# An encoder's first layer on Trainium2: the order of TensorE's instructions, once the planner's, is written out by hand

## The chip, the cores and the metric

The kernel runs on one core of a Trainium2 chip. The metric is the device time of one execution in microseconds (us). It was run three times, and once more with the hardware profiler, whose page and trace the sections below quote. A core has a matrix engine (TensorE, PE in the profile; its weight loads are listed apart as PEld), VectorE (DVE), ScalarE (ACT), GpSimd (POOL), the queues of SyncE (SP), from which all DMA transfers of this kernel are issued, and on-chip memory: SBUF, and PSUM, into which TensorE writes its products.

## What is computed

Two layers of a streaming encoder for one prompt of 1024 tokens and, beside it, 32 tokens of a second stream (the "sample") that has 512 cached keys and values. The width is 1024. Only the first layer is touched:

```python
# h: rmsnorm(x); proj = h @ w_in, 3072 columns: u, q, k, v, g_pool, g_att, 512 each
pool_out = scale * group_map(trailing_mean(u, 2 | 4 | 8 | 16) - u)   # 4 groups of 128 channels
# 8 heads of 64; chunks of 64 queries, each sees its own chunk and the 8 before it
s = einsum('cqhd,ckhd->hcqk', qc, kb) * 64 ** -0.5
s = where(key_chunk >= 0, s + bias[clip(distance, -128, 128)], -inf)
att = einsum('hcqk,ckhd->cqhd', softmax(s), vb)
mixed = concatenate([pool_out * silu(g_pool), att * silu(g_att)])
x = x + rmsnorm(mixed @ w_out)
...
# second layer: an mLSTM with matrix memory, chunk by chunk
```

## The kernel before

Everything is 32-bit. To multiply at TensorE's faster rate without losing accuracy, each operand of a projection is split into a high and a low part of 12 bits, and `mm3` (L99 to L108) adds three products: high by high (L106), low by high (L107) and high by low (L108). Channels lie on the partitions, tokens on the free axis, in three groups of 384, 384 and 288. A **step** is one tile of 128 output channels for one token group: 24 products into one PSUM tile `pd`, which has 3 buffers, and then an evacuation on VectorE or ScalarE. A **tile** of weights is three steps. It is loaded one tile ahead by `load_w`: a DMA into `wr`, the high part on ScalarE (L93), the low part in the first layer on GpSimd (L94), later on VectorE (L94).

The first layer (`layer0`) begins with the input's norm and the projections v and q of the first pair of heads. Then a loop runs over four pairs of heads (L628 to L663). In each pair, in the order of the program:

- what is left of the projection steps queued before (`fill_all`);
- `v_tokens` (L274): the values are turned to have tokens on the partitions, in nine transposes (L288) of a 128 by 128 block, four to a PSUM tile `pm` or `pv`; ScalarE (L289) copies each with a factor to the tile `vt`. Stores and loads of values go with it;
- stacked queries, the projection of the keys (three steps), stacked keys KA and KB, the near bias B;
- the gate `ga` (one buffer; evacuation L268: VectorE, ScalarE's tanh, VectorE), three steps;
- `PLAN` queues the projections v, q, u (pooling input) and gp (pooling gate) that come next, nine or twelve steps a pair;
- scores `att_s` for the two heads (e) and the two halves of the 1024 queries (hf). Scores of key block by queries are two products (L342, L343) into a PSUM tile `ps` (three buffers); two smaller key blocks share one tile (a bank). VectorE adds the near bias (L347), ScalarE the far one (L355). The result stands in `st` (four buffers). Then the maximum over the keys: VectorE's maxima (L363 to L371), an all-reduce over the partitions on GpSimd (L373), a subtraction on VectorE (L377) and the exp on ScalarE (L378);
- values `att_pv` (L388) into `pv` (one buffer), four products for the first half and eight for the second, taken out by ScalarE (L396, L397); behind the second head `att_out`: times the gate on GpSimd (L408), a reciprocal (L409) and a product on VectorE, and a store to `mix` in DRAM;
- the sample's own attention (`rest`, L425 to L462): scores into `ps`, the same steps of a softmax (all-reduce L441, exp L444), five values products (L454; the profile lists each twice, as it does those of L388 and L495) for each head into `pv`, each head's part read by VectorE (L456, L457), a transpose (L459) and a product with the gate.

Behind a tile u stand the trailing sums (`pool_sums`, GpSimd L477, VectorE L481 and L483), behind a tile gp the pooling product (`pool_mix`: L495 for three token groups on one PSUM tile `pm`, each read by VectorE, L497). The output projection (`out_proj`) reads `mix` back, splits the rows (L196) and follows.

None of this order is fixed on the engines. The whole is scheduled by a planner that simulates the kernel's time line and, on each engine, puts next what is ready by its reckoning, with earlier program text first. So projection steps lie among the attention's instructions in TensorE's queue wherever the planner put them, within a step too.

Of the kernel before, what the change touches and what calls it, by code (L numbers as in the profile page):

```python
# [33 lines left out]
class Net:  # L34
# [5 lines left out]
    # ---------------------------------------------------------------- consts  # L40
    def consts(self):
# [4 lines left out]
        # the table of the activations, before the data is there  # L46
# [24 lines left out]
    # keeps [s, t] with s <= t  # L71
# [4 lines left out]
    # ---------------------------------------------------------------- dense  # L76
# [40 lines left out]
    # the same, one token group at a time, to be put between other work; "make" gives evac when the tile starts  # L117
# [26 lines left out]
    # r = 1/sqrt(sum/1024 + eps), on all partitions, from per-partition sums; worked out with the tokens on the partitions  # L144
# [44 lines left out]
    # split x * g into two parts of 12 bits  # L189
# [15 lines left out]
    # the input: one group's tokens, with tiles that are not in use yet for what comes in  # L205
# [23 lines left out]
    # ---------------------------------------------------------------- layer 0  # L229
# [32 lines left out]
    # (1 + tanh(g/2)) * g, twice the silu  # L262
# [11 lines left out]
    def v_tokens(self, vT, pr):  # L274
# [8 lines left out]
        for b0 in (0, 4, 8):  # L283
# [6 lines left out]
        for e in range(2):  # L290
            c0 = pr * 128 + e * 64
            cs = slice(e * 128, e * 128 + 64)
            nc.sync.dma_start(out=io["vo"][0:512, c0:c0 + 64].rearrange("(b p) c -> p b c", p=128), in_=vt[:, 4:8, cs])
            nc.sync.dma_start(out=io["vo"][512:544, c0:c0 + 64], in_=vt[:DEC, 8, cs])
        return vt

    # hi and lo of both heads, stacked on the partitions
# [21 lines left out]

    def att_s(self, pr, e, hf, Q, KA, KB, B):  # L320
# [7 lines left out]
        for group in banks:  # L328
# [32 lines left out]
        mx = self.lp.tile([128, 512], F32, name="mx", bufs=2)  # L361
        if hf == 0:
            nc.vector.tensor_copy(out=mx[:, 0:128], in_=place[0][0][:, 0:128])  # L363
            nc.vector.tensor_tensor(out=mx[:, 128:512], in0=place[0][0][:, 128:512], in1=place[1][0], op=ALU.max)
            rest = [2, 3]
        else:
            nc.vector.tensor_tensor(out=mx, in0=place[3][0], in1=place[4][0], op=ALU.max)
            rest = [2, 1, 0, 5, 6, 7]
# [855 lines left out]
```

## Time and profile before

| | |
|---|---|
| time, three runs | 1272.14 us (median), 1271.83 to 1279.22 |
| span of the profiled execution | 1273.6 us, 19526 instructions |
| TensorE busy | 1200.1 us (94%) |
| TensorE's weight loads | 1148.3 us (90%), beside the products |
| VectorE, ScalarE, GpSimd busy | 688.7 (54%), 471.5 (37%), 316.3 us (25%) |
| DMA | 94.03 MB, mean 74 GB/s |
| chain that ended last | PE 77%, DVE 6%, issue 5%, DMA 5%, POOL 3%, ACT 2% |

The runs' times are the device's; the span is that of one execution under the profiler, and all rows further down are of that one. The chain that ended last is followed back from the last instruction to what released it, and so on; "issue" in it is time in which an engine waited for nothing that the profile shows. The first layer, to its output projection, fills some 460 us.

### The profile page before, as it was taken

How to read it: one execution, taken by the hardware profiler on the slowest of the kernel's cores; microseconds unless marked ns; L12 is line 12 of the kernel's file. 1: busy time of each engine (PE TensorE's matmuls, PEld its weight loads, DVE VectorE, ACT ScalarE, POOL GpSimd, SP SyncE). 2: the span in 40 equal slices, each digit the busy share in tenths (PEclk: the TensorE clock that was granted, in tenths of full speed). 3: DMA queues.
4: the chain of work that ended last, by engine and by line, in shares of the span. 5: the costliest groups of instructions: out<-in, count | busy, mean ns of one | idle time of the engine just before them, and what ended most of it. 6: DMA issues, size and time to landing. Idle time of an engine off the chain costs nothing.

```text
span 1273.6 us, 19526 instructions
## 1 busy us (share of the span) xinstructions
PE 1200.1 (94%) x7457; PEld 1148.3 (90%) x7457; DVE 688.7 (54%) x1457; ACT 471.5 (37%) x976; POOL 316.3 (25%) x409
## 2 busy tenths in 40 slices
PE   6998898978997979999999999999999999999996
PEld 6997797977897859999999989999999999998996
DVE  7654474564676644777435643574237532567324
ACT  6532333243443335543033423343224322346421
POOL 3222532342234223552010320021002210123232
PEclk9998988989999989999999989999999999999998
DMA  6311120111120225332111132113111311113323
GB/s 216 114 38 33 44 85 26 51 59 34 64 71 22 78 85 168 100 127 83 49 51 53 37 71 97 38 49 95 46 50 51 76 68 50 42 60 122 127 99 124
DMA packets 79613, 94.03 MB, mean 74 GB/s; under 512 B 19208, under 2 KB 56856, under 8 KB 79520
## 3 DMA queue, kind: packets, MB, share of 16 engines
q1 hardware_dynamic: 79520, 92.79, 23.5%
q8 instruction: 58, 0.95, 0.3%
q14 instruction: 35, 0.29, 0.1%
HBM read 72.64 MB, written 21.69 MB: 74 GB/s over the span
## 4 chain that ended last, share of the span: by engine, by line
PE 77%; DVE 6%; issue 5%; DMA 5%; POOL 3%; ACT 2%; SPq 0%; DVEq 0%; POOLq 0%; ACTq 0%
PE pd L107 20%; PE pd L106 20%; PE pd L108 20%; PE pv L388 3%; DMA xr<-mix 2%; PE pm L883 1%; PE ps L951 1%; PE ps L343 1%; PE ps L342 1%; POOL qT L477 1%; DMA wr<-in_w0o 1%; POOL wl L94 1%; PE pv L918 1%; DMA MA<-mdr 1%; PE pv L920 1%
## 5 line engine op out<-in xcount | busy, mean ns | idle before, releaser
L106 PE MATMUL pd<-xh,wh 128*128 128x384 f32 (+1 forms) x1864 | 613.6, 330 | 13.5 <-DVE ga L268 6.8
L107 PE MATMUL pd<-xl,wh 128*128 128x384 f32 (+1 forms) x1864 | 612.8, 329 | 13.9 <-POOL xl L196 9.5
L108 PE MATMUL pd<-xh,wl 128*128 128x384 f32 (+1 forms) x1864 | 612.7, 329 | 1.7 <-DVE wl L94 1.6
L107 PEld LDWEIGHTS pd<-xl,wh 128*128 128x128 f32 x1864 | 356.1, 191 | 19.1 <-POOL xl L196 10.2
L106 PEld LDWEIGHTS pd<-xh,wh 128*128 128x128 f32 x1864 | 356.2, 191 | 18.2 <-ACT wh L93 7.6
L108 PEld LDWEIGHTS pd<-xh,wl 128*128 128x128 f32 x1864 | 356.0, 191 | 5.2 <-DVE wl L94 3.0
L93 ACT CAST wh<-wr 128x512 fp32r<-128x512 f32 x158 | 91.4, 618 | 149.6 <-PE pd L107 122.4
L94 DVE TENSOR_TENSOR wl<-wr,wh 128x512 fp32r<-128x512 f32 x116 | 80.5, 718 | 23.7 <-ACT wh L93 22.1
L94 POOL TENSOR_TENSOR wl<-wr,wh 128x512 fp32r<-128x512 f32 x42 | 57.8, 1392 | 116.8 <-ACT wh L93 59.6
L187 POOL TENSOR_TENSOR acc<-acc,sqt 128x384 f32<-128x384 f32 (+1 forms) x48 | 56.6, 1178 | 92.2 <-ACT sqt L186 87.8
L388 PE MATMUL pv<-st,vt 128*128 128x512 f32 (+1 forms) x192 | 58.7, 448 | 0.2 <-ACT st L378 0.2
L73 POOL TENSOR_SCALAR_AFFINE_SELECT D<-D 128x128 f32<-128x128 f32 (+1 forms) x36 | 11.9, 331 | 180.8 <-ACT D L947 168.1
L388 PEld LDWEIGHTS pv<-st,vt 128*128 128x128 f32 x192 | 36.2, 195 | 20.7 <-issue 12.4
L963 POOL TENSOR_TENSOR qa<-qT,MA 128x128 f32<-128x128 f32 (+1 forms) x64 | 27.1, 441 | 107.1 <-DMA MA<-mdr 68.4
L965 POOL TENSOR_TENSOR qal<-qa,qah 128x256 fp32r<-128x256 f32 (+1 forms) x32 | 27.0, 847 | 103.9 <-ACT qah L964 91.6
L347 DVE TENSOR_TENSOR st<-ps,B 128x256 f32<-128x256 f32 (+1 forms) x72 | 26.1, 377 | 45.0 <-PE ps L343 44.4
L377 DVE TENSOR_TENSOR st<-st,mb 128x512 f32<-128x512 f32 (+1 forms) x96 | 40.0, 485 | 15.7 <-POOL mb L373 14.1
L256 DVE TENSOR_TENSOR row<-pd,r 128x384 f32<-128x384 f32 (+1 forms) x36 | 18.6, 521 | 54.4 <-PE pd L108 54.2
L983 DVE SCALAR_TENSOR_TENSOR C<-C,MA,ps 128x258 f32<-128x258 f32 x64 | 30.4, 478 | 32.2 <-PE ps L920 19.0
L373 POOL PARTITION_ALL_REDUCE mb<-mx x16 | 28.8, 1799 | 66.5 <-issue 25.2
L378 ACT ACTIVATE st<-st 128x1280 f32<-128x1280 f32 x24 | 30.4, 1272 | 31.2 <-DVE st L377 31.1
L355 ACT ACTIVATE st<-ps,far 128x256 f32<-128x256 f32 (+3 forms) x56 | 25.6, 487 | 38.9 <-DVE st L347 35.8
(306 smaller groups left out, 1675.8 us busy)
## 6 DMA issues: line engine op xcount, KB each, us to landing
wr<-in_w SPq DMA_DIRECT2D x128, 256.0 KB, 2.7
xr<-mix SPq DMA_DIRECT2D x26, 192.0 KB, 2.9
wr<-in_w0o SPq DMA_DIRECT2D x16, 256.0 KB, 3.1
MA<-mdr SPq DMA_DIRECT2D x32, 128.0 KB, 3.2
wr<-in_w1o SPq DMA_DIRECT2D x16, 256.0 KB, 3.2
x<-in_x SPq DMA_DIRECT2D x16, 192.0 KB, 2.8
x<-x1d SPq DMA_DIRECT2D x16, 192.0 KB, 3.8
out_y<-y SPq DMA_DIRECT2D x16, 192.0 KB, 2.1
```

Source lines behind the costliest of these rows:

```text
L93: nc.scalar.copy(out=wh[:, k], in_=wr)
L94: eng.tensor_tensor(out=wl[:, k], in0=wr, in1=wh[:, k].bitcast(F32), op=ALU.subtract)
L106: nc.tensor.matmul(out=p, lhsT=wh[:, k], rhs=xh[:, k], start=first and i == 0, stop=False)
L107: nc.tensor.matmul(out=p, lhsT=wh[:, k], rhs=xl[:, k], start=False, stop=False)
L108: nc.tensor.matmul(out=p, lhsT=wl[:, k], rhs=xh[:, k], start=False, stop=last and i == len(ks) - 1)
L187: (eng or nc.gpsimd).tensor_tensor(out=acc, in0=acc, in1=t[:, :n], op=ALU.add)
L373: nc.gpsimd.partition_all_reduce(mb, mx, 128, bass_isa.ReduceOp.max)
L377: nc.vector.tensor_tensor(out=dst, in0=dst, in1=mb[:, a - q0:b - q0], op=ALU.subtract)
L378: nc.scalar.activation(out=st, in_=st, func=AF.Exp)
L388: nc.tensor.matmul(out=pv[:, a - q0:b - q0], lhsT=vt[:, j, 64 * e:64 * e + 128], rhs=dst, start=(i == 0), stop=(i == len(order) - 1))
L963: nc.gpsimd.tensor_tensor(out=qa[:, d, :L], in0=qT[:, d, t], in1=Ab, op=ALU.mult)
L983: nc.vector.scalar_tensor_tensor(out=Cn[:, d], in0=C[:, d], scalar=Ab[:, L - 1:L], in1=pu, op0=ALU.mult, op1=ALU.add)
```

## The change

The order of TensorE's instructions in the loop over the pairs is now the order of the program: the loop stands in a `manual_schedule` for that engine. The other engines are still ordered by the planner. To give the program a useful order, the loop's body becomes a method `pair`, which runs projection steps one at a time (`dense_steps`, called `D`) between pieces of the attention. `v_tokens` hands back a function `turn(b0)` for the transposes of up to four blocks, `att_s` a list of steps, one for each `st` tile (one in the first half, two in the second), and the sample's attention is cut into `scores` and `values`. The second half's values (`first`, `second`) run in the next pair, between its key and gate steps. The pooling product is put off by two steps behind its gate tile (`due`; group 0 by none). Nothing is added to or taken from the arithmetic. Comments are stripped in the same diff; those lines are left out here.

```diff
...
-        for b0 in (0, 4, 8):
+        def turn(b0):
             p = self.pv.tile([128, 512], F32, name="pv") if b0 == 4 else self.pm.tile([128, 512], F32, name="pm")
...
+            if b0 == 8:
+                for e in range(2):
...
+                    nc.sync.dma_start(out=io["vo"][512:544, c0:c0 + 64], in_=vt[:DEC, 8, cs])
+        return vt, turn
...
-        for group in banks:
+        def scores(group):
...
+        def soft():
+            mx = self.lp.tile([128, 512], F32, name="mx", bufs=2)
...
+        def step(i):
+            scores(banks[i])
+            if i == len(banks) - 1:
+                soft()
+        return place, [lambda i=i: step(i) for i in range(len(banks))]
...
-        def rest():
+        def scores():
...
+            box["ss"] = ss
+        def values():
+            ss = box["ss"]
...
-        return rest
+        return scores, values
...
+    def dense_steps(self, n):
+        for _ in range(n):
+            if not self.fills:
+                return
+            self.fill()
+            for d in self.due:
+                d[0] -= 1
+            while self.due and self.due[0][0] < 0:
+                self.due.pop(0)[1]()
+    def pair(self, pr, take, xs, rows, do, before, Kc, GA):
+        nc, D = self.nc, self.dense_steps
...
+        D(99)
+        qT = rows["q", pr]
+        Q = self.stacked(qT, "qa")
+        self.later(lambda: take(Kc + pr), xs, make_k)
+        self.later(lambda: take(GA + pr), xs, make_ga)
+        before = list(before)
+        D(1)
+        if before:
+            before.pop(0)()
+        D(2)
+        kT = box["kT"]
...
+        KA = self.stacked(kT, "ka")
+        KB = self.swapped(KA, "kb")
...
+        D(2)
+        if before:
+            before.pop(0)()
+        vt, turn = self.v_tokens(rows["v", pr], pr)
+        D(1)
+        gate = box["gate"]
+        s_scores, s_values = self.att_sample(pr, qT, kT, vt, B, gate)
+        for f, g in PLAN[pr]:
+            do[f](g)
+        n = len(self.fills)
...
+        p00, s00 = S(0, 0)
+        p01, s01 = S(1, 0)
+        p10, s10 = S(0, 1)
+        p11, s11 = S(1, 1)
+        s_scores()
+        s00[0]()
+        turn(0)
+        turn(4)
+        D(1)
+        s01[0]()
+        turn(8)
+        D(1)
+        s10[0]()
+        D(1)
+        s10[1]()
+        D(1 if n == 9 else 2)
+        od0 = self.att_new()
+        self.att_pv(0, 0, p00, vt, od0)
+        D(1)
+        self.att_pv(1, 0, p01, vt, od0)
+        self.att_out(pr, od0, 0, 512, gate)
+        s11[0]()
+        D(1)
+        s11[1]()
+        D(1)
+        s_values()
+        box["od"] = None
+        def first():
+            box["od"] = self.att_new()
+            self.att_pv(0, 1, p10, vt, box["od"])
+        def second():
+            self.att_pv(1, 1, p11, vt, box["od"])
+            self.att_out(pr, box["od"], 512, 1024, gate)
+        return [first, second]
...
-            self.later(lambda: take(GP + g), xs, make, lambda: self.pool_mix(g, pools["u", g], pools["gp", g]))
-        for pr in range(NPAIR):
-            self.fill_all()
...
+            self.later(lambda: take(GP + g), xs, make,
+                       lambda: self.due.append([0 if g == 0 else 2, lambda: self.pool_mix(g, pools["u", g], pools["gp", g])]))
+        self.due = []
+        last = []
+        with tc.manual_schedule(engines={mybir.EngineType.PE}):
+            for pr in range(NPAIR):
+                last = self.pair(pr, take, xs, rows, dict(u=do_u, gp=do_gp, v=do_v, q=do_q), last, Kc, GA)
+            self.dense_steps(2)
+            last[0]()
+            self.dense_steps(99)
+            last[1]()
+            while self.due:
+                self.due.pop(0)[1]()
         yield
-        self.fill_all()
...
```

## Rows read from the trace of the kernel before

**Rows 1.** TensorE's waits: engine, tile, line waited for: total us, times, longest

```profile
PE pv L454 <- ACT ss L444: 20.4, 4, 6.1
PE pd L107 <- POOL xl L196: 9.5, 1, 9.5
PE pd L106 <- DVE ga L268: 6.8, 1, 6.8
...
PE pm L495 <- DVE u L483: 6.5, 2, 5.5
```

**Rows 2.** Busy us by stretch, seven stretches; before the DMA share: granted clock

```profile
456.09:466.33 10.24, 5.99 (x14) 4.15 (x14) 3.34 (x6) 2.83 (x5) 2.98 (x3) 0.50 0.47 135
sum 51.20, PE 36.21 PEld 32.38 DVE 33.61 ACT 13.95 POOL 16.26; mean PE 5.17 PEld 4.63 DVE 4.80 ACT 1.99 POOL 2.32
```

**Rows 3.** Timeline of GpSimd: start, us, instruction [idle before <- what ended it]

```profile
68.29 2.54 POOL L94 TENSOR_TENSOR wl<-wr,wh 128x512 fp32r<-128x512 f32 x2 [9.38 <-ACT wh L93]
...
99.60 0.54 POOL L441 PARTITION_ALL_REDUCE smb<-sm  x1 [6.41 <-issue]
...
103.32 1.78 POOL L373 PARTITION_ALL_REDUCE mb<-mx  x1 [3.17 <-DVE mx L371]
```

**Rows 4.** Timeline of TensorE: first products of two steps, 288 tokens and the next

```profile
137.50 0.29 PE L106 MATMUL pd<-xh,wh 128*128 128x288 f32 x1
...
140.68 0.34 PE L106 MATMUL pd<-xh,wh 128*128 128x384 f32 x1
```

**Rows 5.** The page: a group of instructions (busy, mean ns), a DMA issue

```profile
L378 ACT ACTIVATE st<-st 128x1280 f32<-128x1280 f32 x24 | 30.4, 1272 | 31.2 <-DVE st L377 31.1
...
wr<-in_w SPq DMA_DIRECT2D x128, 256.0 KB, 2.7
```

**Rows 6.** Timeline of TensorE: transposes and the first scores of a pair

```profile
51.66 0.27 PE L288 MATMUL pm<-ident,row 128*128 128x128 f32 x1
...
54.85 0.27 PE L288 MATMUL pm<-ident,row 128*128 128x128 f32 x1
...
67.47 0.39 PE L342 MATMUL ps<-qa,kb 128*128 128x512 f32 x1
...
68.11 0.34 PE L343 MATMUL ps<-qa,ka 128*128 128x384 f32 x1
...
72.16 0.22 PE L342 MATMUL ps<-qa,kb 128*128 128x128 f32 x1
```

**Rows 7.** Timelines of ScalarE and VectorE beside rows 6

```profile
51.97 0.37 ACT L289 ACTIVATE vt<-pm,rcol 128x128 f32<-128x128 f32 x1 [0.99 <-PE pm L288]
...
68.13 0.78 DVE L347 TENSOR_TENSOR st<-ps,B 128x256 f32<-128x256 f32 x2
```

**Rows 8.** Timeline of TensorE: the sample's values, the two heads of a pair

```profile
101.56 1.42 PE L454 MATMUL pv<-vt,ss 128*32 128x65 f32 x10 [4.30 <-ACT ss L444]
...
108.91 0.87 PE L454 MATMUL pv<-vt,ss 128*32 128x65 f32 x10
```

**Rows 9.** Timelines of ScalarE and VectorE around rows 8

```profile
101.04 0.47 ACT L444 ACTIVATE ss<-ss 128x320 f32<-128x320 f32 x1 [10.69 <-DVE ss L443]
...
103.70 0.27 DVE L457 TENSOR_SCALAR so<-pv,srec 32x64 f32<-32x64 f32 x1
...
113.09 0.26 DVE L457 TENSOR_SCALAR so<-pv,srec 32x64 f32<-32x64 f32 x1
```

**Rows 10.** Timelines of TensorE, GpSimd and VectorE: a head's values and what follows

```profile
117.24 2.42 PE L388 MATMUL pv<-st,vt 128*128 128x512 f32 x8
...
120.36 1.29 POOL L408 TENSOR_TENSOR ro<-ro,ga 128x512 f32<-128x512 f32 x1 [5.38 <-ACT ro L396]
...
120.95 3.34 DVE L409 RECIPROCAL rg<-rg 128x512 f32<-128x512 f32 x1
```

**Rows 11.** Timelines of TensorE and VectorE: a pooling product and its reading

```profile
160.68 1.65 PE L495 MATMUL pm<-u,wm 128*128 128x384 f32 x2 [5.53 <-DVE u L483]
...
164.27 0.52 DVE L497 SCALAR_TENSOR_TENSOR gp<-pm,hscale,gp 128x384 f32<-128x384 f32 x1
```

More of the change, by code (lines that the diff above doesn't have):

```diff
@@ L360, in att_s @@
                 off += w
[L361 to L368, printed above, removed]
-        for j in rest:
-            dst, a, b = place[j]
-            nc.vector.tensor_tensor(out=mx[:, a - q0:b - q0], in0=mx[:, a - q0:b - q0], in1=dst, op=ALU.max)
@@ L372, in att_s @@
-        mb = self.lp.tile([128, 512], F32, name="mb", bufs=1)
-        nc.gpsimd.partition_all_reduce(mb, mx, 128, bass_isa.ReduceOp.max)
-        for st, js in tiles:
-            for j in js:
-                dst, a, b = place[j]
-                nc.vector.tensor_tensor(out=dst, in0=dst, in1=mb[:, a - q0:b - q0], op=ALU.subtract)
-            nc.scalar.activation(out=st, in_=st, func=AF.Exp)
-        return place
+        def soft():
+            mx = self.lp.tile([128, 512], F32, name="mx", bufs=2)
+            if hf == 0:
+                nc.vector.tensor_copy(out=mx[:, 0:128], in_=place[0][0][:, 0:128])
+                nc.vector.tensor_tensor(out=mx[:, 128:512], in0=place[0][0][:, 128:512], in1=place[1][0], op=ALU.max)
+                rest = [2, 3]
+            else:
+                nc.vector.tensor_tensor(out=mx, in0=place[3][0], in1=place[4][0], op=ALU.max)
+                rest = [2, 1, 0, 5, 6, 7]
+            for j in rest:
+                dst, a, b = place[j]
+                nc.vector.tensor_tensor(out=mx[:, a - q0:b - q0], in0=mx[:, a - q0:b - q0], in1=dst, op=ALU.max)
+            mb = self.lp.tile([128, 512], F32, name="mb", bufs=1)
+            nc.gpsimd.partition_all_reduce(mb, mx, 128, bass_isa.ReduceOp.max)
+            for st, js in tiles:
+                for j in js:
+                    dst, a, b = place[j]
+                    nc.vector.tensor_tensor(out=dst, in0=dst, in1=mb[:, a - q0:b - q0], op=ALU.subtract)
+                nc.scalar.activation(out=st, in_=st, func=AF.Exp)
@@ L423, in att_sample @@
             nc.vector.tensor_copy(out=qd[64 * e:64 * e + 64, e], in_=qT[64 * e:64 * e + 64, SEQ:T])
-        def rest():
+        box = {}
+        def scores():
             p = self.ps.tile([128, 512], F32, name="ps")
@@ L499, in pool_mix, with make_k, make_ga, S @@
                 nc.sync.dma_start(out=self.mix[128 * g:128 * g + 128, s:s + n], in_=mo)
+    def dense_steps(self, n):
[9 more added lines that the diff above has]
+        nc, D = self.nc, self.dense_steps
+        kT = None
+        box = {}
+        def make_k():
+            box["kT"] = self.row()
+            return self.scaled(box["kT"])
+        def make_ga():
+            box["gate"] = self.lp.tile([128, T], F32, name="ga", bufs=1)
+            return self.gated(box["gate"])
+        D(99)
[9 more added lines that the diff above has]
+        kT = box["kT"]
+        nc.sync.dma_start(out=self.io["ko"][128 * pr:128 * pr + 128], in_=kT[:, 512:T])
+        KA = self.stacked(kT, "ka")
+        KB = self.swapped(KA, "kb")
+        B = self.lp.tile([128, 2, 256], F32, name="B", bufs=1)
+        for e in range(2):
+            src = self.ext[2 * pr + e, 0:1, 128:129]
+            nc.sync.dma_start(out=B[:, e], in_=bass.AP(tensor=src.tensor, offset=src.offset, ap=[[383, 128], [1, 256]]))
+        nc.gpsimd.memset(B[64:128, :, 0:64], NEG)
+        D(2)
[8 more added lines that the diff above has]
+        n = len(self.fills)
+        def S(e, hf):
+            return self.att_s(pr, e, hf, Q, KA, KB, B)
+        p00, s00 = S(0, 0)
[32 more added lines that the diff above has]
+        return [first, second]
```

42 lines of the change are left out of this document (3 added, 39 removed).

## The prediction, made before the change was run

> **What bounds the kernel now.** I read the list of TensorE's waits first, then the granted clock around the long ones, then the timelines of the other engines beside them. TensorE is busy 94% of the span, so a gain must come from its idle stretches or from its clock. In the first layer, behind its input norm, four waits stand out [rows 1]: the sample's values (L454) wait 20.4 us in four places for the exp of the sample (L444); the first product of the output projection waits 9.5 us for a row split on GpSimd; a gate projection waits 6.8 us for an evacuation on VectorE; the pooling product (L495) waits 6.5 us in two places for VectorE. Together 43.2 us. After each long one the granted clock was 0.50, the lower of TensorE's two levels, for 6.8 to 10.2 us; in these seven stretches, 51.20 us, TensorE was busy 36.21 us [rows 2]. At the full level that work takes half, so 18.1 us go there. Waits and aftermath cost 43.2 + 18.1 = 61.3 us of the profiled span of 1273.6 us. That is what an order of TensorE without waits could give back; its work stays the same.
>
> Behind the sample's wait stands GpSimd. Its sample all-reduce starts at 99.60 after 6.41 us in which it waits for nothing that the profile shows; the next all-reduce, 1.78 us, has no such part before it [rows 3]. I read the 6.41 us as the change from the elementwise program to the all-reduce's.
>
> **What the change removes.** The sample's scores now stand ahead of the first head's scores, and its values behind the last scores, eight projection steps later (seven in the pairs with nine steps). A step of 288 tokens takes 3.18 us (137.50 to 140.68 [rows 4]), one of 384 tokens by the same rate 4.24 us, three of a tile 11.7 us, so the distance is 27 to 31 us, against a chain of 6.4 (GpSimd's change), 0.5 for the all-reduce [rows 3] and short pieces on two engines: the 20.4 us go. For a head the distance is four or five steps, 15 to 20 us, with the other head's scores beside them. Its chain is 6.4 + 1.8 [rows 3], some 2 us of subtractions (an estimate) and an exp of 1.27 us [rows 5]: under 12 us behind the evacuation of its scores. No wait there, and still less for the later half, whose values come in the next pair. The pooling product stands two steps behind its gate, about 8 us later than now: its 6.5 us go. The 9.5 us at the end go too: the last all-reduce is then some six steps ahead of the output projection, and GpSimd has changed back when it must split rows. The 6.8 us at the gate go from there, but see A2. All 61.3 us leave their places.
>
> **What it adds.** TensorE's queue is now strictly the written order, and the planner can no longer put projection products between a product and an evacuation that the next product needs. In the old trace it did so in each of these places; each becomes a wait.
>
> A1, transposes. `turn(0)` and `turn(4)` are eight transposes in a row, four to a PSUM tile, and ScalarE reads each one before the next may write the same tile. In the old trace two transposes into one tile start at 51.66 and 54.85, with projection products between, though one lasts 0.27 us [rows 6]. The round trip: transpose start 51.66 to the start of its read 51.97 is 0.31 us, the read 0.37 us [rows 6, 7], ScalarE's end to TensorE's start 0.05 us (101.51 to 101.56 [rows 8, 9]): 0.73 us. Six of the eight wait, and the read of the second tile's first waits for ScalarE too: 7 x 0.73 = 5.1 us, where eight alone cost about 1.1 us (half of 0.27 each, as they overlap, an estimate). 4.0 us a pair with ScalarE free, 16 us in all; up to 5.5 a pair, 22, where score evacuations stand between.
>
> A2, the first head's scores. In front of them the sample's scores hold one of three PSUM tiles, so the last bank waits for the sample's evacuation; and the product over the fourth key block waits for VectorE's read of the second block in its bank (now it starts at 72.16, the other ended at 68.45 [rows 6]). With VectorE free that is 0.8 us. For pairs 1 to 3 it isn't free. The last values of the pair before now stand between the second and third gate step; there is one gate tile, so the new gate's evacuations wait until the old pair's output is multiplied by the old gate (1.29 us on GpSimd), and by then VectorE has begun a reciprocal of 3.34 us, which starts 1.3 us behind the values [rows 10]. From the values' end: 1.3 + 3.3, then five parts of the gate's evacuations and the output product at about 0.55 (0.52 is such a part at 164.27 [rows 11]): 7.9 us. The last gate step (3.2), the sample's scores (1 us, an estimate) and the first bank (0.5) cover 4.7: 3.2 us are left, and 0.8 for the read itself, 4.0. Ends 0.8 and 4.6; as the planner may place the reciprocal elsewhere, I take the middle, 2.7, for three pairs and 0.8 for the first: 9 us.
>
> A3, the same wait in the other three places of a pair where two key blocks share a bank and VectorE reads the first. The product that ended at 68.45 was read by 68.91 [rows 6, 7]; with the hops and the pipeline's overlap (half of 0.34) 0.75 us with VectorE free, up to 1.5 behind a queue. Twelve places, 9 us (9 to 18).
>
> A4, the sample's values. The second head's ten products wait for VectorE's readings of the first's, and the transpose for those of the second. Old trace: products' end 102.98 to the reading's end 103.97, 1.0 us; 109.78 to 113.35, 3.6 us, with other work in VectorE's queue [rows 8, 9]. Least 0.55 twice, most 1.0 + 3.6; I take 2.0 a pair, nearer to the first row as TensorE stands still and so feeds VectorE nothing: 8 us (4 to 18).
>
> A5, the pooling products: three groups on one PSUM tile, so two wait for VectorE. Old trace: 162.33 to 164.79, 2.5 us with VectorE's queue full, of which 0.52 is the read [rows 11]. I take 1.0 each: 8 us for four groups (5 to 18).
>
> A6, the clock. A1 and A2 stand behind each other: some 7 to 9 us a pair in which TensorE does two microseconds of work. The nearest rows are the seven half-clock stretches, all after idle time; one cost 18.1/7 = 2.6 us. Nothing if sparse work keeps the clock, 3.4 us a pair (half of 6.8) where a whole stretch falls on dense steps: I take 1.5, 6 us (0 to 14). A7, the start of the output projection, whose first rows can be split only when the last step of the first token group is done: 0 to 5, taken 2.
>
> Moved at no price: four stores of values (now behind `turn(8)`) and the load of the old keys (now behind the gate; its tile has been free for a pair) pass weight loads in SyncE's queue. A load lands in 2.7 us [rows 5]; each weight load has a tile of 11.7 us as cover. If the keys were issued only at their use they would cost 2.7 us a pair, which is inside A2's upper end. Weight splits on GpSimd (2.54 us [rows 3]) are asked for three steps ahead and stand, as now, in front of the all-reduces.
>
> The added sum is 16 + 9 + 9 + 8 + 8 + 6 + 2 = 58 us, 38 to 110 by the ends. 61.3 - 58 = 3.3 us of gain on the span of 1273.6: 1270.3. The three runs have a median of 1272.14, 1.5 below the profiled span; the same step from there is **1269 us**.
>
> At one place the Trainium skill speaks against the change. The rows show no stretch in which transposes stand nearly alone, so they cannot say what the clock does there. "TensorE: Matmul & The Clock Gate", section "Part 4: PE-mode transpose", says that a transpose doesn't count as busy for the clock gate as other products do. By that rule, which no run here shows, the clock falls in every pair.
>
> **The rivals.** First, faster: the waits come out at their lower ends, because VectorE and ScalarE, 54% and 37% busy, get through their queues while TensorE stands, and grouped scores and transposes save TensorE some changes of kind between projection products (5 us, an estimate). 38 to 50 us are added: 1272 - 61 - 5 + 38 = 1244, and 1256 with 50, say 1250. For it: most single hops above are short. Against it: rows 9 and 11, where VectorE's queue doubled or trebled the price.
>
> Second, slower: the wait for the all-reduce isn't removed but moves into the transposes. ScalarE runs its queue in order, and the planner doesn't know GpSimd's 6.4 us. If the exps of the sample and of the first head stand ahead of the last reads of the transposes, TensorE waits in `turn(4)` for them: the weight split ended 3.4 us behind the first scores (70.83 against 67.47 [rows 3, 6]), then 6.4, all-reduces of 0.5 and 1.8, subtractions 2, exp 1.3: 15.4 us behind the gate step, where A1 and A2 end at about 8 (first pair) to 12. 3 to 7 us a pair and longer at the low clock, 22 us more in all: 1291. It decides from the point where one such read stands behind the first head's exp. For it: in the old trace ScalarE idled 10.69 us in front of the sample's exp [rows 9], so its queue can be held there. Against it: the transposes are ready early.
>
> Third, the skill's rule as a mechanism of this kernel: each pair's run of transposes leaves the low clock on dense steps, 4 x 3.4 = 13.7 instead of 6: 1277.
>
> That the change doesn't do what it says, TensorE's order staying the planner's, gets no more than 1 in 50; it would be 1272.
>
> **How the numbers follow.** 1% is 12.7 us, about what a measurement of this kernel can tell from no change. The forecast with the third rival and the empty change, within 1%: 0.38. The first rival, faster by over 1%: 0.36. The second (0.18) and a heap of upper ends without it (0.08), slower by over 1%: 0.26. The range takes the first rival down to 1243 and the second up to 1300.
>
> **What would show it.** No wait of L454 for the exp any more; new waits at L288 for L289 (16 us), at the scores for L347, at L454 and L459 for L457, at L495 for L497; the clock low once a pair beside the transposes. If ScalarE's exp holds the queue that ends the wait at L288, the second rival holds. If L288's wait is under 8 us, two blocks of a bank aren't ordered as I read it, and the first holds. The prediction fails as a whole if the new waits are of another kind, weights for instance.

## The result, and the profile after

The changed kernel takes 1338.99 us in the median of four runs (1336.82 to 1340.98), the kernel before in four runs 1271.99 us. The ratio is 1.0507, with a 95% interval of 1.0473 to 1.0541: 67 us slower, where 1269 us and at most 1300 had been forecast.

The page of the changed kernel, its span, the busy time by engine and the chain that ended last:

```profile
span 1335.1 us, 19529 instructions
...
PE 1225.3 (92%) x7457; PEld 1162.5 (87%) x7457; DVE 681.9 (51%) x1457; ACT 474.6 (36%) x976; POOL 311.7 (23%) x409
...
PE 76%; DVE 9%; issue 5%; DMA 4%; ACT 3%; POOL 2%; SPq 0%; DVEq 0%; POOLq 0%; ACTq 0%
```

TensorE runs as many instructions as before (7457), yet is busy 25 us longer, and its idle time has grown by 36 us (span less busy, 73.5 before, 109.8 after). The place is the loop over the pairs. From the first product of the first pair's gate to the same product of the output projection, 528 high-by-high products (L106) apart in both, the two kernels take 424.25 and 481.72 us, 57.5 of the 61.5 us between the spans. Busy times by stretch for these two, before first (columns: length, then busy us and instructions of PE, PEld, DVE, ACT and POOL, granted clock, DMA share, GB/s):

```profile
55.47:479.72 424.25, 380.79 (x2158) 348.41 (x2157) 247.88 (x475) 156.19 (x274) 132.43 (x131) 0.94 0.18 55
```

```profile
55.81:537.53 481.72, 403.28 (x2162) 358.12 (x2161) 244.16 (x477) 161.68 (x279) 127.91 (x131) 0.89 0.16 50
```

TensorE's waits in that stretch of the changed kernel, to be held against [rows 1]:

```profile
PE ps L346 <- DVE st L351: 22.2, 16, 3.3
PE pv L289 <- ACT vt L290: 19.4, 12, 4.2
PE ps L346 <- ACT st L359: 9.8, 3, 3.8
PE pm L289 <- ACT vt L290: 6.4, 12, 0.9
PE pv L471 <- DVE so L474: 5.4, 4, 3.3
PE pm L512 <- DVE gp L514: 4.3, 6, 0.7
PE pv L399 <- ACT rg L408: 3.7, 1, 3.7
...
PE ps L476 <- DVE so L474: 2.6, 4, 0.6
```

Lines have moved: the transposes and their reading (L288, L289) are now L289 and L290, scores L346 and L347, their readings L351 (VectorE) and L359 (ScalarE), a head's all-reduce, subtraction and exp L379, L383 and L384, its values L399, their copies L407 and L408 and the reciprocal L420, the sample's all-reduce, exp, values and transpose L454, L457, L471 and L476, the pooling product L512. The reader is to see two things. The four waits of 43.2 us in [rows 1] are gone, as forecast; 0.2 us are left of the one at the pooling product. And 78.6 us of waits stand there now, nearly all of them (the eight rows shown, 73.8 us) for VectorE or ScalarE to read a PSUM tile; 4.6 us of weights at the output projection are the largest rest.

The low clock has become the other half. The first of ten stretches at 0.50 in this part, and the sum of the ten, against [rows 2]:

```profile
72.10:85.75 13.65, 7.22 (x22) 5.43 (x21) 4.48 (x15) 4.73 (x11) 2.33 (x2) 0.50 0.14 37
...
sum 102.38, PE 65.06 PEld 55.17 DVE 53.91 ACT 35.64 POOL 23.85; mean PE 6.51 PEld 5.52 DVE 5.39 ACT 3.56 POOL 2.38
```

TensorE was busy 65.06 us at half speed, where it had been 36.21: half of it, 32.5 us, is the price, 14.4 more than before.

Where a wait comes from is seen best in the second pair. TensorE's timeline, transposes behind the first head's scores (start, us, instruction, idle time before and what ended it):

```profile
193.58 0.27 PE L289 MATMUL pm<-ident,row 128*128 128x128 f32 x1
194.31 0.33 PE L289 MATMUL pm<-ident,row 128*128 128x128 f32 x1 [0.46 <-ACT vt L290]
...
196.76 0.42 PE L289 MATMUL pv<-ident,row 128*128 128x128 f32 x1
200.96 0.47 PE L289 MATMUL pv<-ident,row 128*128 128x128 f32 x1 [3.79 <-ACT vt L290]
```

ScalarE beside it:

```profile
199.92 0.47 ACT L457 ACTIVATE ss<-ss 128x320 f32<-128x320 f32 x1 [3.49 <-DVE ss L456]
...
200.55 0.36 ACT L290 ACTIVATE vt<-pv,rcol 128x128 f32<-128x128 f32 x1
```

And GpSimd:

```profile
198.55 0.54 POOL L454 PARTITION_ALL_REDUCE smb<-sm  x1 [6.59 <-issue]
```

The transpose at 200.96 waits for ScalarE's copy of the one before it, whose product was done by 197.18 (196.76 and 0.42). But the copy starts at 200.55, as the sample's exp stands in front of it in ScalarE's queue; the exp waits for VectorE's subtraction, this for the all-reduce, and the all-reduce for 6.59 us in which GpSimd waits for nothing that the profile shows. That is the second rival's chain.

The later half's scores are the place that the prediction lacked. GpSimd, ScalarE, TensorE and VectorE, second pair:

```profile
234.34 1.80 POOL L379 PARTITION_ALL_REDUCE mb<-mx  x1 [6.03 <-issue]
```

```profile
237.97 1.28 ACT L384 ACTIVATE st<-st 128x1280 f32<-128x1280 f32 x1 [7.55 <-DVE st L383]
239.57 1.27 ACT L384 ACTIVATE st<-st 128x1280 f32<-128x1280 f32 x1 [0.33 <-DVE st L383]
...
242.08 1.52 ACT L359 ACTIVATE st<-ps,far 128x512 f32<-128x512 f32 x3
```

```profile
242.82 0.80 PE L346 MATMUL ps<-qa,kb 128*128 128x512 f32 x1 [2.80 <-ACT st L359]
...
247.97 0.48 PE L346 MATMUL ps<-qa,kb 128*128 128x128 f32 x1 [3.29 <-DVE st L351]
```

```profile
242.09 3.35 DVE L420 RECIPROCAL rg<-rg 128x512 f32<-128x512 f32 x1 [1.94 <-ACT rg L408]
...
247.51 0.41 DVE L351 TENSOR_TENSOR st<-ps,B 128x256 f32<-128x256 f32 x1
```

The scores of the second head, computed at 236 us, are read by ScalarE only at 242.08. In front of this reading stand two exps of the first head, which wait for an all-reduce with 6.03 us of nothing before it, and the two copies of the second head's values for the first half. The next two-block tile waits for a reading that VectorE begins at 247.51, behind the reciprocal and the product that follows it.

### The profile page after: what moved, and what is told of

Its sections match the earlier page's. It is cut to its first block, busy times and chain, and to the rows that moved or that the text cites. A ratio compares the mean times of both kernels' runs of the same rounds, so it can differ in the third digit from the quotient of the medians.

```text
span 1335.1 us, 19529 instructions
## 1 busy us (share of the span) xinstructions
PE 1225.3 (92%) x7457; PEld 1162.5 (87%) x7457; DVE 681.9 (51%) x1457; ACT 474.6 (36%) x976; POOL 311.7 (23%) x409
## 4 chain that ended last, share of the span: by engine, by line
PE 76%; DVE 9%; issue 5%; DMA 4%; ACT 3%; POOL 2%; SPq 0%; DVEq 0%; POOLq 0%; ACTq 0%
PE pd L106 20%; PE pd L107 20%; PE pd L108 20%; PE pv L399 3%; DMA wr<-in_w0o 1%; DVE st L383 1%; DMA xr<-mix 1%; PE pm L968 1%; PE ps L1036 1%; DVE st L351 1%; PE ps L346 1%; PE pv L1003 1%; PE pv L1005 1%; DVE xl L202 1%; PE pv L1004 1%
## 5 line engine op out<-in xcount | busy, mean ns | idle before, releaser
L106 PE MATMUL pd<-xh,wh 128*128 128x384 f32 (+1 forms) x1864 | 616.6, 331 | 7.9 <-ACT wh L93 7.9
L106 PEld LDWEIGHTS pd<-xh,wh 128*128 128x128 f32 x1864 | 358.7, 193 | 10.3 <-ACT wh L93 8.4
L94 POOL TENSOR_TENSOR wl<-wr,wh 128x512 fp32r<-128x512 f32 x42 | 55.0, 1324 | 94.8 <-issue 43.1
L346 PE MATMUL ps<-qa,kb 128*128 128x512 f32 (+1 forms) x96 | 35.4, 380 | 32.0 <-DVE st L351 22.2
L383 DVE TENSOR_TENSOR st<-st,mb 128x512 f32<-128x512 f32 (+1 forms) x96 | 40.0, 485 | 45.2 <-POOL mb L379 45.2
L399 PE MATMUL pv<-st,vt 128*128 128x512 f32 (+1 forms) x192 | 56.7, 447 | 3.7 <-ACT rg L408 3.7
L384 ACT ACTIVATE st<-st 128x1280 f32<-128x1280 f32 x24 | 30.5, 1273 | 76.0 <-DVE st L383 76.0
L399 PEld LDWEIGHTS pv<-st,vt 128*128 128x128 f32 x192 | 35.8, 195 | 24.0 <-issue 12.7
L346 PEld LDWEIGHTS ps<-qa,kb 128*128 128x128 f32 x96 | 19.9, 207 | 40.0 <-DVE st L351 27.9
L379 POOL PARTITION_ALL_REDUCE mb<-mx x16 | 28.7, 1794 | 97.3 <-DVE mx L377 56.1
L351 DVE TENSOR_TENSOR st<-ps,B 128x256 f32<-128x256 f32 (+1 forms) x72 | 25.7, 373 | 41.0 <-PE ps L347 40.9
```

The source lines that it names most:

```text
L94: eng.tensor_tensor(out=wl[:, k], in0=wr, in1=wh[:, k].bitcast(F32), op=ALU.subtract)
L106: nc.tensor.matmul(out=p, lhsT=wh[:, k], rhs=xh[:, k], start=first and i == 0, stop=False)
L346: nc.tensor.matmul(out=p[:, w:w + n], lhsT=KB[e][:, ks], rhs=Q[e][:, a:b], start=True, stop=False)
L351: nc.vector.tensor_tensor(out=dst[:, :m], in0=p[:, w:w + m], in1=B[:, e, ra:ra + m], op=ALU.add)
L379: nc.gpsimd.partition_all_reduce(mb, mx, 128, bass_isa.ReduceOp.max)
L383: nc.vector.tensor_tensor(out=dst, in0=dst, in1=mb[:, a - q0:b - q0], op=ALU.subtract)
```

## The experiments

Three theories were set against each other. **Q (queues)**: TensorE's fixed order stops wherever the reading that it needs stands, in the in-order queue of ScalarE or VectorE, behind something slow, above all behind an all-reduce that has to wait for GpSimd's change of program. **P (program)**: the rearranged program is slow in any order. **C (clock)**: the low clock comes from the kind of work, transposes and scores in a row, and not from waits. All runs are against the kernel before on the same chip, 1273.5 to 1275.3 us in the median (1271.99 for the changed kernel), so a difference between two rows of the table is good to some 2 or 3 us.

| run | median us | ratio to before, 95% interval |
|---|---|---|
| changed kernel | 1338.99 | 1.0507 [1.0473, 1.0541] |
| 1 planner orders the changed program | 1277.65 | 1.0019 [0.9998, 1.0041] |
| 2 transposes ahead of the scores | 1339.37 | 1.0510 [1.0491, 1.0528] |
| 3 transposes inside the gate step | 1311.05 | 1.0273 [1.0245, 1.0301] |
| 4 both blocks ahead of the reading | 1322.80 | 1.0372 [1.0342, 1.0402] |
| 5 GpSimd runs all-reduces and fills only | 1305.78 | 1.0245 [1.0210, 1.0281] |
| 6 late reciprocals | 1331.47 | 1.0451 [1.0412, 1.0490] |
| 7 runs 3 and 4 together | 1290.40 | 1.0130 [1.0085, 1.0176] |
| 8 all waits of the order treated | 1261.45 | 0.9893 [0.9859, 0.9928] |
| 9 runs 8 and 5 together | 1245.07 | 0.9775 [0.9747, 0.9802] |
| 10 kernel before with run 5's edit | 1237.88 | 0.9714 [0.9689, 0.9740] |
| 11 run 8, longer distances | 1245.87 | 0.9792 [0.9752, 0.9831] |
| 12 runs 11 and 5 together | 1242.05 | 0.9746 [0.9719, 0.9773] |

**Run 1, the order alone undone.**

```diff
-        with tc.manual_schedule(engines={mybir.EngineType.PE}):
+        with nullcontext():
```

> The changed program as it is, but TensorE is ordered by the planner again, like the other engines. Theory Q (queues): the loss comes from TensorE standing in a fixed order behind instructions of ScalarE and VectorE which themselves stand behind others in those engines' queues; with the planner free to put projection products there it is gone: 1260 to 1290 us. Theory P (program): the new program itself costs the time, whatever the order on TensorE, for instance by the later half's values that are carried into the next pair: above 1320 us.

It came out at the time before: theory P falls, and the 67 us are the price of the written order on TensorE, with what it does to the other engines. The planner's order isn't without waits either: it has 10.4 us at the values for the exp, 9.3 us at the scores for L359 and 5.9 us at the values for L408.

**Run 2, the transposes moved ahead.**

```diff
-        s_scores()
-        s00[0]()
         turn(0)
         turn(4)
+        s_scores()
+        s00[0]()
         D(1)
```

> The eight transposes of turn(0) and turn(4) stand ahead of the sample's scores instead of behind the first head's. Theory Q: the four waits of 3.6 to 4.2 us for a read of the transposes, 15.7 us in all, are waits for the sample's exp in front of that read in ScalarE's queue; they go, and with them a piece of the low clock; the round trips of 0.46 us stay: 1339 - 16 - 4 = 1319 us. Rival R (round trip): the waits belong to the round trip of transposes that stand in a row, wherever that is, or the exp holds another reader as long: within 5 us of 1339.

The waits of 3.6 to 4.2 us at the transposes went, as theory Q said (the longest is now 1.3 us), and the time didn't move, as the rival said. TensorE, GpSimd and VectorE in the second pair show why:

```profile
212.31 0.33 PE L346 MATMUL ps<-qa,kb 128*128 128x128 f32 x1 [3.16 <-DVE st L351]
```

```profile
204.76 0.54 POOL L454 PARTITION_ALL_REDUCE smb<-sm  x1 [6.01 <-issue]
```

```profile
210.23 1.70 DVE L383 TENSOR_TENSOR st<-st,mb 128x512 f32<-128x512 f32 x4 [0.96 <-POOL mb L379]
211.84 0.42 DVE L351 TENSOR_TENSOR st<-ps,B 128x256 f32<-128x256 f32 x1
```

The same chain from GpSimd now ends at the next reader: the sample's all-reduce is late by 6.01 us and the head's all-reduce follows it, VectorE's subtractions wait for that one, and the reading that the second head's scores need stands behind them. The theory was right on the cause and wrong on what moving the victim would bring.

**Run 3, the transposes put among a step's products.** A list of calls, `hooks`, is taken up one by one behind each key slice of a step.

```diff
+            if self.hooks:
+                self.hooks.pop(0)()
...
         vt, turn = self.v_tokens(rows["v", pr], pr)
+        self.hooks = [f for two in zip(turn(0), turn(4)) for f in two]
         D(1)
...
         s00[0]()
-        turn(0)
-        turn(4)
```

> The eight transposes stand between the products of the last gate step, one behind each of its eight key slices and alternately into two PSUM tiles. Theory Q: all waits of L289 go (25.8 us), some 8 us in which transposes stand alone too, and the low clock beside them, about 6 us more: 1339 - 40 = 1299 us. Theory C (clock by kind): the transposes themselves bring the clock down, so that it is as low in each pair as before: about 1308 us, and low stretches of the old length at the gate step.

28 us came back. 1311.05 us is 12 us above theory Q's figure and 3 above theory C's, so the time alone would speak for C. The trace doesn't: the sign that C had named, a low clock at the gate step, is missing. The full clock is granted through the gate steps of all four pairs with their eight transposes; the second pair's:

```profile
177.40:182.50 5.10, 4.72 (x39) 4.50 (x37) 3.53 (x2) 3.98 (x10) 2.03 (x2) 1.00 0.23 51
```

What theory Q lacked lies elsewhere: of the 25.8 us of waits at the transposes 1.1 are left, but the waits at the scores for VectorE rose from 22.2 to 30.2 us. Again a part moved on.

**Run 4, two blocks of a tile computed before the first is read.** The loop over the blocks is cut in two, products in one and readings in the next.

```diff
                     nc.tensor.matmul(out=p[:, w:w + n], lhsT=KA[e][:, ks], rhs=Q[e][:, a:b], start=False, stop=True)
+                    w += n
+                w = 0
+                for j in js:
+                    dst, a, b = place[j]
+                    n = b - a
                     ra = a - 128 * j
```

> Where two key blocks share a PSUM tile, both are computed before VectorE and ScalarE read the first. Theory Q: the 16 waits of L346 for L351 (22.2 us) go, less some 4 us where the next wait (for a free tile) comes up behind, and with them 3 to 5 us of low clock: 1339 - 22 = 1317 us. Rival: the wait is for a free tile and not for the first block's reading, so it stays: within 5 us of 1339.

16 us. The 22.2 us for L351 are gone entirely, so the wait was the one that the prediction had named (A2 and A3); against that the wait for a free tile rose from 9.8 to 17.5 us and the sample's values from 5.4 to 12.1 us:

```profile
PE ps L346 <- ACT st L364: 17.5, 8, 3.9
PE pv L476 <- DVE so L479: 12.1, 4, 3.8
```

**Run 5, the root.** Weight splits, the product with the gate and the trailing sums go from GpSimd to VectorE; fills and all-reduces stay.

```diff
-        nc.gpsimd.tensor_tensor(out=o[:, :n], in0=o[:, :n], in1=gate[:, q0:q1], op=ALU.mult)
+        nc.vector.tensor_tensor(out=o[:, :n], in0=o[:, :n], in1=gate[:, q0:q1], op=ALU.mult)
...
-            nc.gpsimd.tensor_tensor(out=dst[:, lo:L], in0=src[:, lo:L], in1=src[:, lo - sh:L - sh], op=ALU.add)
+            nc.vector.tensor_tensor(out=dst[:, lo:L], in0=src[:, lo:L], in1=src[:, lo - sh:L - sh], op=ALU.add)
...
-        self.weng = nc.gpsimd
+        self.weng = nc.vector
```

> The changed order, with GpSimd's elementwise work of the first layer (weight splits, the product with the gate, trailing sums) on VectorE, so that GpSimd runs all-reduces and fills alone and need not change its program. Theory Q with GpSimd's change as its root: all-reduces start some 6 us earlier, so nothing stands long behind them in VectorE's and ScalarE's queues; the waits at the transposes (15.7 us) go with their share of low clock, about 1339 - 16 - 6 = 1317 us, or less if other waits hang on it too. Rival V (VectorE's load): VectorE takes some 50 us more and its queue is what TensorE waits for, so that as much comes back: 1335 to 1350 us.

33 us, more than expected. GpSimd's waits that nothing in the profile explains, first in the changed kernel's stretch, then in run 5 as a whole:

```profile
POOL wl L94 <- issue: 43.1, 6, 7.7
POOL mb L379 <- issue: 29.6, 5, 6.0
POOL smb L454 <- issue: 26.1, 4, 7.0
```

```profile
POOL acc L187 <- issue: 10.8, 1, 10.8
POOL smb L454 <- issue: 6.4, 1, 6.4
POOL D L73 <- issue: 5.7, 1, 5.7
```

From 15 in the loop to one, at its beginning (the 10.8 and 5.7 us lie outside it). So the 6 us in front of an all-reduce belong to elementwise work on the same engine. The edit also takes that work itself off GpSimd (127.9 us busy in the stretch, 46.7 in run 5), and no run separates the two. The first pair speaks for the gap: there it stayed, with nothing but a fill on GpSimd since the loop began, and a wait at the transposes stayed with it:

```profile
74.47 0.54 POOL L454 PARTITION_ALL_REDUCE smb<-sm  x1 [6.38 <-issue]
```

```profile
76.94 0.48 PE L289 MATMUL pv<-ident,row 128*128 128x128 f32 x1 [3.88 <-ACT vt L290]
```

With the other gaps went the waits for L359 (9.8 us) and L408 (3.7 us) at the later half's scores and values, and 10.5 of the 25.8 us at the transposes; VectorE's longer queue gave back 3.8 us at the sample's values. The rival on VectorE's load falls.

**Run 6, VectorE's long instruction.**

```diff
+            with self.tc.issue_after(after) if after is not None else nullcontext():
                 nc.vector.reciprocal(out=d[:, :n], in_=d[:, :n])
...
         s11[1]()
+        late0(self.rd)
```

Here `rd` is the last reading of the scores; the last values of the pair before are treated alike behind `s00[0]`.

> The changed order, with each reciprocal of 3.35 us and the product behind it put in VectorE's queue behind the last reading of the scores that follow. Theory Q with VectorE's long instruction as the cause: the waits of 2.5 to 3.3 us for L351 at the later half's scores and most of those of 2.2 us at the first head's go, 9 + 4 us, with some 4 us of low clock: 1322 us. Rival A (ScalarE): the exps and copies in ScalarE's queue hold the same scores as long, so that less than 6 us come back: 1333 us or more.

7.5 us, nearer to the rival. The wait for L351 fell from 22.2 to 16.3 us and the untouched transposes' from 25.8 to 16.9, that for ScalarE's L359 stayed (10.6), and 6 us came up at the sample's values and transpose. The reciprocal is one of several things in front of the readings.

**Run 7, runs 3 and 4 together.**

> The third and the fourth run's edits together: transposes inside the gate step, both key blocks of a tile ahead of their reading. They took 28 and 16 us off alone. If each removes its own waits: 1295 us. If a wait that is removed in one place comes up at the next reader of the same queues, as in the second run: above 1303 us.

49 us, where the two alone made 28 and 16: run 4's edit takes away the waits at the scores for VectorE, to which a part of run 3's had moved on. Some 21 us of waits at the scores for ScalarE are left.

**Run 8, every wait of the order treated.** To run 7 and run 6 come: both heads' products of the sample's values ahead of their readings, the sample's transpose and the pooling products as hooks in the steps behind, and a step between the first half's values and the later half's scores.

```diff
+            for e in range(2):
                 v0, d0 = (0, 64) if e == 0 else (1, 0)
...
+            self.hooks += [lambda: None, lambda: None, turned]
...
+        for s, n in GR:
+            self.hooks += [lambda: None, lambda s=s, n=n: part(s, n)]
...
+        D(1)
         s11[0]()
```

> All edits that keep the written order but take its waits away: transposes inside the gate step, both blocks ahead, late reciprocals, both heads of the sample's values ahead of their reading and its transpose inside the next step, the pooling products inside a step, and one more projection step between the first half's values and the later half's scores. Theory Q: from 1295 us the waits of L471, L476 and L512 (12 us), of the reciprocals (13 us) and their low clock go: 1265 to 1272 us, the time before the change or a little under. Theory C (the clock falls with the kind of work and not with waits): 1285 us or more, with low stretches left beside scores and values.

The written order is now 1.1% faster than the kernel before, some 4 us under theory Q's range and far from theory C's 1285. Scores and values still stand together as they did, with few of their waits; eight of a pair's nine transposes stand inside the gate step, as in run 3. The gate step of the second pair:

```profile
168.19:173.19 5.00, 4.63 (x37) 4.29 (x36) 2.19 (x5) 4.35 (x12) 2.03 (x2) 1.00 0.23 52
```

The full clock is granted through it, and so it is through the scores behind, to 184 us. In the loop five low stretches are left of ten, with a quarter of their time:

```profile
sum 27.31, PE 21.47 PEld 20.18 DVE 18.28 ACT 6.80 POOL 11.31; mean PE 4.29 PEld 4.04 DVE 3.66 ACT 1.36 POOL 2.26
```

For scores and values theory C falls, and for transposes among projection products too. For transposes in a row it isn't tested: no run has them so without waits.

**Run 9, run 8 with GpSimd's elementwise work on VectorE** (run 5's edit).

> The eighth run's kernel with GpSimd's elementwise work of the first layer on VectorE, as in the fifth run. Theory Q with GpSimd's change of program as the root of what is left: in the eighth run 15.5 us are left at the sample's transpose and 8.4 us at the scores, some of it behind all-reduces; half of it goes, with its low clock: 1245 to 1252 us. Rival V: those are waits for VectorE's own queue, which now has 50 us more work: 1258 to 1275 us.

1245.07 us. The waits at the scores fell from 8.4 to 2.0 us, and one of 3.3 us for an evacuation on VectorE went; the sample's transpose, which I had counted in, kept 14.4 of its 15.5 us. The time is the one expected; the places are so only in part.

**Run 10, the kernel before with run 5's edit.** Nothing of the change is in it.

> The kernel before, whose TensorE is ordered by the planner, with the same work moved from GpSimd to VectorE. Theory Q: the planner's order too lost its time to GpSimd's changes of program: the 20.4 us of L454 go for the most part, with four or five of the seven low stretches at 2.6 us: 1273 - 18 - 12 = 1243 us. Rival: the planner's model of all-reduces is what keeps its order fitting whatever GpSimd does, and VectorE's queue takes the place of GpSimd's: 1265 to 1280 us.

1237.88 us, the fastest kernel of the study, 2.9% under the one before. TensorE's waits in the same stretch of the program, whole list:

```profile
PE pd L107 <- POOL xl L196: 8.2, 1, 8.2
PE pd L108 <- DVE wl L94: 2.2, 1, 2.2
PE pd L106 <- ACT wh L93: 2.1, 1, 2.1
PE pv L288 <- ACT vt L289: 1.1, 4, 0.3
```

Of the waits of [rows 1] only the one at the output projection stands. The sample's all-reduce, which had 6.41 us of nothing before it in [rows 3], now waits for its data alone:

```profile
93.32 0.52 POOL L441 PARTITION_ALL_REDUCE smb<-sm  x1 [2.22 <-DVE sm L440]
```

**Run 11, longer distances in run 8.**

```diff
-            self.hooks += [lambda: None, lambda: None, turned]
+            self.hooks += [lambda: None] * 12 + [turned]
...
-        self.hooks = [f for two in zip(turn(0), turn(4)) for f in two]
+        self.hooks += [f for two in zip(turn(0), turn(4)) for f in two]
...
         s11[0]()
-        D(1)
+        D(2)
```

> The eighth run's kernel with the sample's transpose one and a half steps behind its values instead of a quarter step, and one more projection step between the two tiles of the later half's scores. Theory Q (a wait of a written order is distance too short for the queue of the engine that it waits for): the 15.5 us of L494 go, and half of the 8.4 us of L352, with the low clock behind them: 1261 - 22 = 1239 us. Rival: VectorE's queue reaches TensorE elsewhere, in the evacuation of the projections: above 1250 us.

16 of the 22 us. The transpose's wait fell from 15.5 to 2.6 us and the scores' from 8.4 to 2.2; 9.9 us appeared at the values (L410), which waited for nothing in run 8; that the stops before them had sheltered them there is argued only.

**Run 12, runs 11 and 5 together.**

> The ninth and the eleventh run's edits together. If GpSimd's changes and short distances are two prices of the same waits: no faster than the eleventh run by more than 5 us. If they add: the eleventh run less 10 us, about 1230 us.

3.8 us under run 11: the two are prices of the same waits. The hand-written order, with all that was found, stays some 4 us behind the planner's with three lines changed (1240.57 to 1243.52 against 1236.89 to 1239.11; the intervals of the ratios overlap).

## Why the prediction was wrong, step by step

| step | forecast us | measured us, changed kernel |
|---|---|---|
| removed: four waits and their low clock | 61.3 | 61.5 (43.4 of waits and 18.1) |
| A1 transposes | 16 | 25.8 |
| A2 first head's scores | 9 | 8.5 (1.88, 2.23, 2.23, 2.15) |
| A3 two blocks in a tile, elsewhere | 9 | 13.7 (22.2 less 8.5) |
| A4 sample's values | 8 | 8.0 (5.4 and 2.6) |
| A5 pooling products | 8 | 4.5 |
| A6 low clock | 6 | 32.5 |
| A7 start of the output projection | 2 | 4.6 (for weights, not for row splits) |
| not in the prediction: later half's scores and values wait for ScalarE | 0 | 13.5 (9.8 and 3.7) |
| not in the prediction: TensorE busy longer at the full clock | 0 | 8.1 |

The last row is what TensorE's busy time grew by, 22.5 us, less the 14.4 of the clock; that it comes from products that stand alone and no longer overlap with others is not shown. The added rows make 119.2 us, more than the 110 of the prediction's upper ends; less 61.5 that is 57.7, against 57.5 measured in the stretch. They must close, as length is busy and idle time: this shows that no wait is left out, not that each has the right cause.

What was removed was right in mechanism and size. A2, A4 and A5 were right in their places and near in size, A2 and A4 in part by luck: A2's first pair waited 1.88 us where 0.8 had been forecast, the others 2.2 where 2.7 had; of A4's 8.0 us 4.0 fell in the last pair and 1.2 to 1.4 in the others, where 2.0 each had been forecast. Run 4 shows A3's mechanism.

**The step that failed most is A6.** It priced the clock at 1.5 us a pair, with one low stretch as its nearest row and 14 us as its end. In the trace each pair has one or two stretches of 10.24 or 13.65 us instead of one of 6.83. Beside the transposes, the only place that the term looked at, they cost 13.8 us (half of the busy time of the four stretches there), at the very end of what it allowed; the other 18.7 us fall where it had nothing: 13.1 around the later half's values and scores, 3.1 at the last pair's sample, 2.5 at the output projection. The waits stand in clusters of short products and stops, and the clock stays low through such a cluster and some way into the dense step behind it. In the first pair the clock falls at 72.10, 0.66 us after the first head's wait of 1.88 us has ended and beside the first transpose; the stops at the transposes follow, and it comes back only at 85.75, 4.3 us into the next step. 26.5 of the 61 us by which the sum missed are this. Where runs took away much of the stretch's idle time (78.4 us in the changed kernel), the low clock (102.4 us) went with it: 61.9 and 71.7 us are left in run 3, 57.5 and 64.9 in run 5, 48.8 and 58.0 in run 7, 32.1 and 27.3 in run 8. Small gains didn't bring it back: runs 2, 4 and 6, with 66.7 to 71.1 us of idle time, have 99.0 to 109.2 us of low clock.

**The second step that failed is a sentence, not a term**: "No wait there", of the heads' values. It reckoned how long the values' own chain takes and covered it with projection steps, and no value waits for its exp. But the prediction didn't ask who stands behind that chain: ScalarE's queue with two exps and VectorE's with a reciprocal, both late by GpSimd's change, hold the readings of the next scores. That is 13.5 us, and 9.0 of A3's 13.7 (three waits of 2.50 to 3.29 us at the later half's scores; the other nine of the twelve places had 0.52 each, under the 0.75 forecast). With the 13.1 us of low clock there, the later half alone is over half of the miss.

**The second rival, with a chance of 0.18, is what happened in A1.** Its condition (a reading of the transposes behind an exp that waits for GpSimd) held in all four pairs, with the sample's exp, at 4.13, 3.79, 4.19 and 3.61 us, 15.7 in all, inside the 3 to 7 us a pair that it was priced at. It gave 1291 us because it added this to a sum that was short by the clock and the later half. Without the exp's 15.7 us A1's waits are 10.1. The round trip itself was 0.73 us from start to start (193.58 to 194.31), as forecast, but 0.94 us at the low clock, where most of the transposes ran.

The third rival, transposes that lower the clock by themselves, stays open. Spread among projection products they don't: the rows of runs 3 and 8 have eight of them in a step with the clock at 1.00. But wherever they stand in a row (the changed kernel, runs 2, 4, 5 and 6) some of each pair's eight run at the low clock, and there they wait too, so that the two can't be told apart. The Trainium skill, "TensorE: Matmul & The Clock Gate", section "Part 4: PE-mode transpose", says that they don't count as busy for the clock as other products do; spread among projection products, no cost of that is seen here, and no run has them in a row without waits.

What is shown and what is argued. Shown: that the fixed order costs the 67 us (run 1), that elementwise work on GpSimd, beside all-reduces, is behind 33 us of it (run 5), that the waits at the transposes and at the two-block tiles are behind 28 and 16 us, overlapping with the first (runs 3, 4 and 7), and that the low clock goes when most of the idle time goes (runs 3, 5, 7 and 8). Argued from the traces alone: that in these 33 us it is GpSimd's changes of program that count and not the work itself, and what part of the low clock beside the transposes is theirs and not the waits'. That the planner puts the exp in front of the copies because it doesn't reckon with GpSimd's 6 us is argued in the same way; no run changed the planner's reckoning.

## What to carry to other kernels

An order written by hand for one engine is only as good as its distance to the readers of its tiles, and these readers sit in the in-order queues of other engines: for each product ask not when its input is ready, but what else stands in front of the instruction that frees its tile. A wait that is moved out of the way of one reader comes up at the next; look for the root that all of them share, here three lines that mixed two kinds of work on GpSimd, before rearranging the victims. And price idle time in clusters by the low clock that comes behind, which here added two fifths to the waits themselves, 32.5 us to 78.6, and look for the clusters at every place where queues of readers are long, not only where the rearranged instructions stand.

## What the runs showed of the hardware

GpSimd's change between elementwise instructions and an all-reduce shows as idle time that ends by "issue": 5.9 us in the mean before a head's all-reduce (29.6 us in five), 6.5 before the sample's (26.1 in four), 7.2 before a weight split (43.1 in six). Fills are free of it: in run 5 they alternate with all-reduces through the whole loop, with one such gap. The Trainium skill, "GPSIMD Engine Reference", section "2.1 Instruction dispatch", gives about 6 us for the first call to a newly loaded kernel; the trace agrees in size, with the means above, but no run shows that the gap is such a load. What I had not expected is its worth: three lines that keep GpSimd to all-reduces and fills in the first layer's loop took 2.9% off a kernel whose GpSimd is 25% busy and stands in TensorE's list of waits for this stretch only once, at the end.
